# Last V slots of a decoder block taken in another order, with their operands prepared further ahead

## The chip, the cores and the metric

One core of a Trainium2 chip runs the whole program. The metric is the device time of one execution in microseconds (us). PE is TensorE, DVE is VectorE, ACT is ScalarE, SP is the queue that issues the plain DMA transfers; POOL issues the gathers.

## The reference, cut to what matters

The program is a decoder block for 512 tokens and 1024 columns. Its second half is a product-key retrieval over 16384 single-neuron experts, followed by a residual sum and a layer norm:

```python
ub = u[eb]
hb = gelu(einsum('pd,ped->pe', xb, ub))
return einsum('pe,ped->pd', (gb * hb), v[eb])
...
x = layer_norm(ALPHA * x + gate2 * y, ln2_g, ln2_b)
```

Each token uses 128 of the 16384 experts. `gb` is the softmax weight of a chosen expert.

## The kernel before, in words

The 512 tokens are four blocks of 128. Block 0 gathers its rows of `u` and `v` and works through them on DVE, one "unit" (one gathered row per token) at a time, into `y`. Blocks 1 to 3 are computed densely. The experts are cut into 128 **slots** of 128 experts. For slot i, PE first multiplies the U rows by the tokens (`u_mm`), ACT applies gelu into a `stash` tile, and 32 slots later (`LOOK`) PE multiplies the weighted activations by the V rows (`v_mm`), accumulating over all slots in six PSUM banks `yb`: three blocks by two halves of 512 columns. So from slot 96 on only V products are left.

A V slot needs operands that `heads` and `prep` make. Every f32 operand is cut into a high and a low part, so each product is three matmuls (high by high, high by low, low by high). For slot i these are:

- `vraw`: 512 KB of V rows, loaded by SP into one of 3 buffers. A load can start when DVE has read the slot three places earlier.
- `wt`: the dense softmax weights of four slots in one 768 KB load, 2 buffers. Slots 120 to 123 are in chunk 30 and slots 124 to 127 in chunk 31.
- ACT makes the high parts: `vhi` or `uhi` from `vraw` (two buffers each, even slots use v, odd ones u, so slot i needs the matmuls of slot i-4 done), and `ghi` from `gt`. The last four slots, 124 to 127, put their V operands into `h2hi` and `h2lo`, which nothing else uses any more.
- DVE makes `gt` (stash times `wt`), then the low parts: `glo` (2 buffers, so slot i needs slot i-2's matmuls done) and `vlo` or `ulo`. The last `GROUP` = 6 slots put both parts of g into tiles called `glast`, cut from the ring of stash tiles, which need no wait for PE.

`prep(i)` first calls `heads(i)` and `heads(i+1)`; the latter puts the `gt` of slot i+1 into DVE's queue ahead of the `glo` and `vlo` of slot i. Each engine works through its queue in the order in which the program wrote it. How far `prep` runs ahead of `v_mm` in that order is set by `ahead(i)`: two slots, and more for the last three slots before the group.

The last six slots are different: instead of going slot by slot over all banks, PE takes one bank's columns (a **piece**) for all six slots, then the next piece, so that the norm of block 1 can begin while PE is still on blocks 2 and 3. The first piece therefore needs the operands of all six slots. `finish(tb)` is the norm of a block: on DVE for block 0 it is written in five parts (a generator `f0`), one part per slot from slot `LAST` = 115 on. After the last piece, DVE finishes block 3 and SP stores it.

Of the kernel before, what the change touches and what calls it, by code (L numbers as in the profile page):

```python
# [9 lines left out]
F32R = mybir.dt.float32r  # L10
# [10 lines left out]
P = 128  # L21
# [3 lines left out]
TB = 4  # L25
HD = 64
NH = 8
NK = 128
# [7 lines left out]
ND = 384  # L36
TG = 32
NTG = ND // TG
LOOK = 32
WR = 4  # L40
# [4 lines left out]
LEAD = 3  # L45
# [7 lines left out]
BIG = 4  # L53
LAST = 115
GROUP = 6
PRE = 0

CW = 80
# [9 lines left out]
def tile_block(ctx, tc, xr, xT, ccol, wada, bcol, brow, wqk, wv, sinks, gncol, wout,  # L68
# [22 lines left out]
    def split(src, hi, lo, eng=None):  # L91
        A.activation(hi, src, AF.Copy)  # L92
        (eng or V).tensor_tensor(lo, src, hi.bitcast(F32), op=OP.subtract)  # L93

    def load_split(src, shape, tag, pool, eng=None, rawtag=None, rawbufs=None):
        raw = pool.tile(shape, F32, name=f"{tag}raw", tag=rawtag or f"{tag}raw", bufs=rawbufs)
        nc.sync.dma_start(raw, src)
        hi = pool.tile(shape, F32R, name=f"{tag}hi", tag=f"{tag}hi")
        lo = pool.tile(shape, F32R, name=f"{tag}lo", tag=f"{tag}lo")
        split(raw, hi, lo, eng)  # L100
        return hi, lo
# [40 lines left out]
    with ExitStack() as front:  # L142
# [92 lines left out]
        heads = []  # L235
# [283 lines left out]
        for g in range(2):  # L519
            for tb in range(TB):  # L520
                T.matmul(p[:, 4 * g + tb:4 * g + tb + 1], sqa[:, g, tb * P:(tb + 1) * P], ones[:, 0:1], start=True,
                         stop=True, skip_group_check=True)
# [26 lines left out]
        for tb in (1, 2, 3, 0):  # L549
            t = slice(tb * P, (tb + 1) * P)  # L550
            zg = [[ps.tile([P, 512], F32, name="zm", tag="ms"[g]) for _ in range(2)] for g in range(2)]
            for n_c, c in enumerate(ORDER):
                hi, lo = wo[c]
# [51 lines left out]
    mw = mw_cm.__enter__()  # L605

    def bank(tag, nm, shape=(P, 512), bufs=None):
        return ps.tile(list(shape), F32, name=nm, tag=tag, bufs=bufs)
# [33 lines left out]
    for hp in range(NHP):  # L642
        hi, lo = load_split(wq[hp].rearrange("p (c n) -> p c n", c=DC), [P, DC, P], "u", wsp, G)
# [217 lines left out]
    def fetch(n):  # L861
        extra = when[n] > NK - LOOK + 1 and n % 3 == 0
        gat[n] = gather(u_rows, n, extra) if n < P else gather(v_rows, n - P, extra)

    def fetch_to(slot):
        while (n := len(gat)) < 2 * P and when[n] <= slot:
            fetch(n)

    def unit(n):
        t = gat[n]  # L870
        if n < P:
            scr = mw.tile([P, D], F32, name="gscr", bufs=1)
            V.tensor_tensor_reduce(out=scr, in0=t, in1=h2row, scale=1.0, scalar=0.0, op0=OP.mult, op1=OP.add,  # L873
                                   accum_out=hd[:, n:n + 1])
            return
        if n == P:
            A.activation(cf, hd, AF.Gelu_apprx_tanh)
            V.tensor_tensor(cf, cf, g0k, op=OP.mult)
        k = n - P
        if k == 0:  # L880
            V.tensor_scalar(y0, t, cf[:, 0:1], None, op0=OP.mult)
        else:
            V.scalar_tensor_tensor(y0, t, cf[:, k:k + 1], y0, op0=OP.mult, op1=OP.add)  # L883

    mw_cm.__exit__(None, None, None)
    mw = ctx.enter_context(tc.tile_pool(name="mv", bufs=2, reuse_waits="tile"))

    ybank = [[bank(f"y{2 * b + h}", f"yb{b}{h}") for h in range(2)] for b in range(3)]
    uraw, vraw, uop, vop, gop, wts = {}, {}, {}, {}, {}, {}
# [4 lines left out]
            nc.sync.dma_start(uraw[s], uT[s])  # L894

    vseen = set()

    def load_v(i):
        if i < NK and i not in vseen:
            vseen.add(i)  # L900
            vraw[i] = mw.tile([P, D], F32, name="vraw", bufs=3)
            nc.sync.dma_start(vraw[i], v_rows[i * P:(i + 1) * P, :])

    def load_w(c):
        if c < NK // WR:
            w = mw.tile([P, NTG, WR, TG], F32, name="wt")
            nc.sync.dma_start(w.rearrange("p g r t -> p g (r t)"),
                              w_d[:, :, c * WR * TG:(c + 1) * WR * TG].rearrange("g p n -> p g n"))
            wts[c] = w

    def hilo(pool, shape, nm, bufs=2):
        return [pool.tile(shape, F32R, name=f"{nm}{e}", tag=f"{nm}{e}", bufs=bufs) for e in ("hi", "lo")]
# [3 lines left out]
    def weigh(i):  # L916
        if i >= NK or i in gts:
            return
        g = mw.tile([P, NTG, TG], F32, name="gt")
        V.tensor_tensor(g, stash.pop(i).rearrange("p (a t) -> p a t", t=TG), wts[i // WR][:, :, i % WR, :], op=OP.mult)  # L920
        gts[i] = g.rearrange("p a t -> p (a t)")
        gop[i] = [mw.tile([P, ND], F32R, name=f"g{e}", tag=f"g{e}", bufs=k) for e, k in (("hi", 3), ("lo", 2))]             if i < NK - GROUP else [
            ring.tile([P, ND], F32R, name="glast", tag="stash") for _ in range(2)]

    def vtiles(i):
        if i >= NK - 4:
            k = 2 * (i - NK + 4)
            vop[i] = [t[:, k:k + 2].rearrange("p a n -> p (a n)") for t in (h2hi, h2lo)]
        else:
            vop[i] = hilo(wsp, [P, D], "u") if i + LOOK > NK and i % 2 else hilo(mw, [P, D], "v")  # L930

    def heads(i):
        if i < NK and i not in gts:
            vtiles(i)
            A.activation(vop[i][0], vraw[i], AF.Copy)
            weigh(i)
            A.activation(gop[i][0], gts[i], AF.Copy)

    def prep(i, units):
        units = list(units)  # L940
        alone = i + LOOK > NK
        if alone:
            heads(i)
            heads(i + 1)
        elif i < NK:
            weigh(i)
            A.activation(gop[i][0], gts[i], AF.Copy)  # L947
        s = i + LOOK
        if s < NK:
            r = uraw.pop(s).rearrange("p (c n) -> p c n", c=DC)  # L950
            uop[s] = hilo(wsp, [P, DC, P], "u")
            split(r, *uop[s])
        if i < NK:
            if not alone:
                vtiles(i)
            V.tensor_tensor(gop[i][1], gts[i], gop[i][0].bitcast(F32), op=OP.subtract)
            if alone:
                V.tensor_tensor(vop[i][1], vraw.pop(i), vop[i][0].bitcast(F32), op=OP.subtract)
            else:
                split(vraw.pop(i), *vop[i])  # L960
        fetch_to(i + (LEAD if i + LOOK >= NK else 1))
        for n in units:
            unit(n)

# [10 lines left out]
    def v_mm(i, b, cols=((0, 512), (512, 1024))):  # L975
        (hi, lo), (ghi, glo) = vop[i], gop[i]
        t = slice(b * P, (b + 1) * P)
        for n, (x, y) in enumerate(((ghi, hi), (ghi, lo), (glo, hi))):
            for c0, c1 in cols:
                T.matmul(ybank[b][c0 // 512][:, c0 % 512:(c1 - 1) % 512 + 1], x[:, t], y[:, c0:c1],  # L980
                         start=(i == 0 and n == 0),
                         stop=(n == 2 and i == (NK - GROUP - 1 if b == TB - 2 else NK - 1)) or c1 - c0 < 512,
                         skip_group_check=(c1 - c0 < 512))

    plan = [[] for _ in range(NK + 1)]
    todo = list(range(PRE, 2 * P))
    for n, t in enumerate(todo):
# [17 lines left out]
    def pieces(tb):  # L1005
        n = 256 if tb == TB - 1 else 512
        return [(c, c + n) for c in range(0, D, n)]
# [32 lines left out]

    for n in range(min(RING, PRE)):
        fetch(n)
    while len(stash) < LOOK:
        u_slot(len(stash), bank("h", "ph", bufs=2), ring.tile([P, ND], F32, name="stash"), V if len(stash) < LOOK - LG else G)
    for n in range(PRE):
        unit(n)
        if n + RING < PRE:
            fetch(n + RING)
# [13 lines left out]
    def ahead(i):  # L1062
        if i + LOOK < NK:
            return i + 1
        return min(i + 2, NK - GROUP - 1) if i < NK - GROUP - 3 else min(NK, 2 * i - (NK - GROUP) + 8)

    for i in range(NK):
        load_u(i + LOOK + 2)
        load_v(i + 3)
        if i + LOOK >= NK:  # L1070
            load_v(i + 4)
        if i % WR == WR - 1:
            load_w(i // WR + 2)
        p = u_mm(i + LOOK) if i + LOOK < NK else None
        if i < NK - GROUP:
            for b in range(3):
                v_mm(i, b)
        while done <= ahead(i):
            prep(done, plan[done])
            done += 1  # L1080
            if i + LOOK >= NK:
                load_v(done + 1)
                load_v(done + 2)
        if p is not None:
            A.activation(stash[i + LOOK], p[:, :ND], AF.Gelu_apprx_tanh)  # L1085
        if i == NK - LOOK + 1:
            A.preload_act_table_set("natural_log_exp_and_others")

        if i == LAST - 2:
            finish_load(0)  # L1090
        if i == LAST:
            f0 = finish(0)
            finish_ln()
        if i >= LAST:
            next(f0, None)
        if i == NK - GROUP - 1:
            for tb in range(1, TB):
                finish_load(tb)
    for _ in f0:
        pass  # L1100
    for b in range(3):
        for c in pieces(b + 1):
            for i in range(NK - GROUP, NK):
                v_mm(i, b, (c,))
        for _ in finish(b + 1):
            pass
# [70 lines left out]
```

## Time and profile before

| what | us |
|---|---|
| median of 3 runs (1597.34 to 1597.96) | 1597.37 |
| the profiled execution | 1595.99 |
| its span, first to last instruction | 1594.3 |
| PE busy in the span (98%) | 1554.9 |
| DVE busy in the span (77%) | 1220.3 |

The span is what the trace shows; the 1.7 us around it belong to the execution's own time. The profiled execution is 1.4 us under the median of the runs.

### The profile page before, as it was taken

What the parts mean: (1) busy time and instruction counts of PE and PEld (TensorE: products, weight loads), DVE (VectorE), ACT (ScalarE), POOL (GpSimd) and SP (SyncE); (2) the same over time, 40 slices, a digit from 0 to 9 for tenths busy, and PEclk for the clock granted to TensorE, in tenths of its full rate; (3) what the DMA queues carried; (4) which work ended last, traced back from release to release, by engine and by line L of the source; (5) the groups of instructions that cost most, each with busy time, mean ns of one, the idle gap of its engine ahead of it and who ended that gap; (6) DMA issues with size and microseconds to landing.
All of it is one profiled execution on the core that took longest, in us unless ns stands there. A gap on an engine that the chain in (4) does not pass through costs nothing.

```text
span 1594.3 us, 21985 instructions
## 1 busy us (share of the span) xinstructions
PE 1554.9 (98%) x8109; PEld 1346.3 (84%) x8109; DVE 1220.3 (77%) x2351; ACT 647.5 (41%) x935; POOL 455.8 (29%) x410
## 2 busy tenths in 40 slices
PE   8999999999989999999999999999999999999996
PEld 5776767788879999899999999999999999998885
DVE  2568585589999997578777787777877777777878
ACT  2535574333355555333333333333333333333331
POOL 0002133544400000233334333333333444333100
PEclk8999898999999999999999999999999999999999
DMA  9564132222225555999888988999889998989873
GB/s 338 184 258 158 53 112 101 79 92 81 81 80 212 219 210 202 334 327 326 305 311 301 326 301 304 306 309 322 302 303 312 307 321 301 311 282 305 261 231 119
DMA packets 147356, 382.12 MB, mean 240 GB/s; under 512 B 11312, under 2 KB 68656, under 8 KB 143280
## 3 DMA queue, kind: packets, MB, share of 16 engines
q1 hardware_dynamic: 110384, 246.49, 44.6%
q0 software_dynamic: 36864, 134.23, 24.4%
q8 instruction: 63, 1.03, 0.3%
q14 instruction: 45, 0.37, 0.1%
HBM read 351.32 MB, written 29.36 MB: 239 GB/s over the span
## 4 chain that ended last, share of the span: by engine, by line
PE 79%; DVE 12%; DMA 3%; ACT 3%; issue 1%; POOL 1%; SPq 0%; DVEq 0%; ACTq 0%; POOLq 0%
PE yb L980 32%; PE ph L970 25%; PE pw L841 5%; PE ph L806 4%; PE pj L303 3%; PE zm L556 2%; DVE scr L620 1%; PE pj L274 1%; DMA wa<-in_wada_dram 1%; DVE tsi L622 1%; DVE tsi L619 1%; PE pq L647 1%; DVE tsv L621 1%; DVE tsv L618 1%; PE oacc L398 1%
## 5 line engine op out<-in xcount | busy, mean ns | idle before, releaser
L855 POOL DMA_INDIRECT gat<-in_u_rows_dram,idx x128 | 161.6, 1262 | 478.5 <-DVE hd L873 226.5
L93 DVE TENSOR_TENSOR ulo<-uraw,uhi 128x1024 fp32r<-128x1024 f32 x133 | 162.5, 1223 | 164.9 <-ACT uhi L92 160.5
L970 PE MATMUL ph<-h2hi,ulo 128*128 128x384 f32 x768 | 258.6, 337 | 0.6 <-DVE ulo L93 0.6
L970 PE MATMUL ph<-h2hi,uhi 128*128 128x384 f32 x768 | 258.2, 336 | 0.3 <-ACT uhi L92 0.3
L970 PE MATMUL ph<-h2lo,uhi 128*128 128x384 f32 x768 | 258.2, 336 | 0.0
L855 POOL DMA_INDIRECT gat<-in_v_rows_dram,idx x128 | 161.0, 1258 | 264.8 <-DVE y L883 224.1
L980 PE MATMUL yb<-vhi,ghi 128*128 128x512 f32 x654 | 203.0, 391 | 0.0
L980 PE MATMUL yb<-vhi,glo 128*128 128x512 f32 x654 | 202.9, 391 | 0.0
L980 PE MATMUL yb<-vlo,ghi 128*128 128x512 f32 x654 | 202.6, 391 | 0.0
L92 ACT ACTIVATE uhi<-uraw 128x1024 fp32r<-128x1024 f32 x155 | 162.4, 1050 | 74.6 <-PE pq L647 52.9
L883 DVE SCALAR_TENSOR_TENSOR y<-gat,cf,y 128x1024 f32<-128x1024 f32 x127 | 162.7, 1281 | 3.9 <-DMA gat<-in_v_rows_dram,idx 1.6
L873 DVE CUSTOM_DVE_ANT_0 gscr<-gat,h2row 128x1024 f32<-128x1024 f32 x128 | 156.5, 1222 | 10.6 <-DMA gat<-in_u_rows_dram,idx 7.9
L1085 ACT ACTIVATE stash<-ph 128x384 f32<-128x384 f32 x96 | 47.2, 491 | 275.1 <-PE ph L970 275.1
L970 PEld LDWEIGHTS ph<-h2lo,uhi 128*128 128x128 f32 x768 | 144.4, 188 | 4.4
L970 PEld LDWEIGHTS ph<-h2hi,uhi 128*128 128x128 f32 x768 | 144.4, 188 | 4.4 <-ACT uhi L92 0.7
L980 PEld LDWEIGHTS yb<-vlo,ghi 128*128 128x128 f32 x654 | 122.7, 188 | 27.3
L980 PEld LDWEIGHTS yb<-vhi,glo 128*128 128x128 f32 x654 | 122.8, 188 | 26.8
L970 PEld LDWEIGHTS ph<-h2hi,ulo 128*128 128x128 f32 x768 | 144.4, 188 | 1.0 <-DVE ulo L93 1.0
L980 PEld LDWEIGHTS yb<-vhi,ghi 128*128 128x128 f32 x654 | 121.8, 188 | 18.9
L93 DVE TENSOR_TENSOR vlo<-vraw,vhi 128x1024 fp32r<-128x1024 f32 x97 | 118.4, 1220 | 17.5 <-ACT vhi L92 17.4
L92 ACT ACTIVATE vhi<-vraw 128x1024 fp32r<-128x1024 f32 x97 | 102.8, 1060 | 53.6 <-issue 35.8
L947 ACT ACTIVATE ghi<-gt 128x384 fp32r<-128x384 f32 x97 | 51.0, 525 | 177.7 <-DVE gt L920 177.7
(311 smaller groups left out, 2860.1 us busy)
## 6 DMA issues: line engine op xcount, KB each, us to landing
uraw<-in_uT_dram SPq DMA_DIRECT2D x128, 512.0 KB, 5.2
vraw<-in_v_rows_dram SPq DMA_DIRECT2D x128, 512.0 KB, 5.2
w_d<-stage SPq DMA_DIRECT2D x12, 2048.0 KB, 7.3
wt<-w_d SPq DMA_DIRECT2D x32, 768.0 KB, 9.3
wa<-in_wada_dram SPq DMA_DIRECT2D x16, 1024.0 KB, 6.5
wah<-in_wada_dram SPq DMA_DIRECT2D x16, 512.0 KB, 9.4
uraw<-in_wq_dram SPq DMA_DIRECT2D x16, 512.0 KB, 3.3
uraw<-in_wqk_dram SPq DMA_DIRECT2D x11, 512.0 KB, 7.8
```

The lines of the kernel that those rows point to most:

```text
L92: A.activation(hi, src, AF.Copy)
L93: (eng or V).tensor_tensor(lo, src, hi.bitcast(F32), op=OP.subtract)
L303: T.matmul(p, a[:, dc], b[:, dc], start=(dc == 0 and n == 0), stop=(dc == DC - 1 and n == 2))
L806: T.matmul(p[:, :ND], a[:, dc], b[:, dc, P:], start=(dc == 0 and n == 0), stop=(dc == DC - 1 and n == 2))
L841: T.matmul(p[:, k * P:(k + 1) * P], oh4[:, 1, :, k], oh4[:, 2 + j, :, k], start=(j == 0), stop=(j == 1), skip_group_check=True)
L855: G.indirect_dma_start(out=t, out_offset=None, in_=rows, in_offset=bass.IndirectOffsetOnAxis(ap=idx[:, k:k + 1], axis=0))
L873: V.tensor_tensor_reduce(out=scr, in0=t, in1=h2row, scale=1.0, scalar=0.0, op0=OP.mult, op1=OP.add, accum_out=hd[:, n:n + 1])
L883: V.scalar_tensor_tensor(y0, t, cf[:, k:k + 1], y0, op0=OP.mult, op1=OP.add)
L947: A.activation(gop[i][0], gts[i], AF.Copy)
L970: T.matmul(p[:, :ND], a[:, dc], b[:, dc, P:], start=(dc == 0 and n == 0), stop=(dc == DC - 1 and n == 2))
L980: T.matmul(ybank[b][c0 // 512][:, c0 % 512:(c1 - 1) % 512 + 1], x[:, t], y[:, c0:c1], start=(i == 0 and n == 0), stop=(n == 2 and i == (NK ...
L1085: A.activation(stash[i + LOOK], p[:, :ND], AF.Gelu_apprx_tanh)
```

## The change

The last six slots are taken in the order 124, 125, 126, 127, 122, 123 (`seq`), both in `prep` and in the pieces. Slots 114 and later (`OWN` = 14 of them) take both parts of g from the stash ring. `ahead` asks for two slots ahead up to slot 113, for four from slot 114 on, and for all that is left by slot 119. Two parts of the norm of block 0 are written per slot. `prep` also loads the weight chunk of its slots if nobody has yet.

```diff
+OWN = 14
+    seq = list(range(NK - GROUP)) + list(range(NK - 4, NK)) + list(range(NK - GROUP, NK - 4))
...
-    def load_v(i):
-        if i < NK and i not in vseen:
+    def load_v(n):
+        i = seq[min(n, NK - 1)]
+        if n < NK and i not in vseen:
...
-            if i < NK - GROUP else [
+            if i < NK - OWN else [
             ring.tile([P, ND], F32R, name="glast", tag="stash") for _ in range(2)]
...
-    def prep(i, units):
+    def prep(n, units):
         units = list(units)
+        i = seq[n] if n < NK else n
         alone = i + LOOK > NK
         if alone:
-            heads(i)
-            heads(i + 1)
+            for k in (n, n + 1):
+                if k < NK:
+                    load_w(seq[k] // WR)
+                    heads(seq[k])
...
-        return min(i + 2, NK - GROUP - 1) if i < NK - GROUP - 3 else min(NK, 2 * i - (NK - GROUP) + 8)
+        if i < NK - OWN:
+            return i + 2
+        return min(i + 4 + 3 * max(0, i - (NK - GROUP - 5)), NK)
...
         if i >= LAST:
             next(f0, None)
+            next(f0, None)
...
-            for i in range(NK - GROUP, NK):
+            for i in seq[NK - GROUP:]:
                 v_mm(i, b, (c,))
```

First place: SP's queue from the load of block 0's residual (`x1b`) on. Before, with the V loads of slots 116 to 118 in the first row, 119 alone, chunk 30, 120, the two norm vectors `ln`, 121 to 123, chunk 31, and 124 to 127:

```order
L902 DMA vraw<-in_v_rows_dram 128x1024 x3
L998 DMA x1b<-x_d 128x1024
L902 DMA vraw<-in_v_rows_dram 128x1024
L907 DMA wt<-w_d 128x12x128
L902 DMA vraw<-in_v_rows_dram 128x1024
L1003 DMA ln_13768<-in_ln2r_dram 128x1024
L1003 DMA ln_13770<-in_ln2r_dram 128x1024
L902 DMA vraw<-in_v_rows_dram 128x1024 x3
L907 DMA wt<-w_d 128x12x128
L902 DMA vraw<-in_v_rows_dram 128x1024 x4
```

The same place now; the V loads are of slots 116 to 118, then 119 to 121, then 124, 125, 126, and last 127, 122 and 123:

```order
L905 DMA vraw<-in_v_rows_dram 128x1024 x3
L1004 DMA x1b<-x_d 128x1024
L905 DMA vraw<-in_v_rows_dram 128x1024 x3
L910 DMA wt<-w_d 128x12x128
L905 DMA vraw<-in_v_rows_dram 128x1024
L1009 DMA ln_13792<-in_ln2r_dram 128x1024
L1009 DMA ln_13794<-in_ln2r_dram 128x1024
L905 DMA vraw<-in_v_rows_dram 128x1024
L910 DMA wt<-w_d 128x12x128
L905 DMA vraw<-in_v_rows_dram 128x1024
L1045 DMA out_dram<-y_2423 128x512 x2
L905 DMA vraw<-in_v_rows_dram 128x1024 x3
```

Chunk 30 has moved behind the V loads of slots 120 and 121, and chunk 31 stands behind that of slot 125, the second of the last six.

Second place: DVE's queue around the `gt` of slot 120, the first that reads chunk 30, with what each row waits for (DMAHW is a load, PE and Activation an engine). Before, from the first part of block 0's norm on (the `gt` of slots 119 and 120 are the second and the seventh row):

```order
L1019 TENSOR_TENSOR y_2423<-y_2423,gate_76 128x1024
L920 TENSOR_TENSOR gt<-stash,wt 128x384 [waits DVE_49]
L956 TENSOR_TENSOR glo<-gt,ghi 128x384 [waits PE_49,Activation_49]
L958 TENSOR_TENSOR vlo<-vraw,vhi 128x1024 [waits DMAHW1_49]
L1029 SCALAR_TENSOR_TENSOR y_2423<-x1b,y_2423 128x512 [waits DMAHW2_49,DVE_49]
L1030 BN_STATS l2st<-y_2423 128x6 [waits DVE_49]
L920 TENSOR_TENSOR gt<-stash,wt 128x384 [waits DMAHW4_49]
L956 TENSOR_TENSOR glo<-gt,ghi 128x384 [waits PE_49,Activation_49]
L958 TENSOR_TENSOR ulo<-vraw,uhi 128x1024 [waits DMAHW3_49]
```

Now (the `gt` of slots 119 and 120 are the first and the fourth row):

```order
L923 TENSOR_TENSOR gt<-stash,wt 128x384 [waits DVE_49]
L962 TENSOR_TENSOR glast<-gt,glast 128x384 [waits Activation_49]
L964 TENSOR_TENSOR vlo<-vraw,vhi 128x1024 [waits DMAHW1_49,PE_49]
L923 TENSOR_TENSOR gt<-stash,wt 128x384 [waits DMAHW6_49,DVE_49]
L962 TENSOR_TENSOR glast<-gt,glast 128x384 [waits Activation_49]
L964 TENSOR_TENSOR ulo<-vraw,uhi 128x1024 [waits DMAHW3_49,PE_49]
L1025 TENSOR_TENSOR y_2423<-y_2423,gate_76 128x1024
L1035 SCALAR_TENSOR_TENSOR y_2423<-x1b,y_2423 128x512 [waits DMAHW2_49,DVE_49]
L1036 BN_STATS l2st<-y_2423 128x6 [waits DVE_49]
```

The low part of g no longer waits for PE, the low part of V now does, and the first part of the norm of block 0 has moved from behind slot 117 to behind slot 119.

Third place: DVE's queue around the first `gt` that reads chunk 31. Now, from the end of the fourth part of the norm of block 0 on, where the `gt` is that of slot 124, the `glast` and `ulo` are those of slot 121, and the last part of the norm of block 0 follows:

```order
L114 TENSOR_TENSOR l2rs<-l2rs,l2tm 128x1 [waits DVE_49]
L923 TENSOR_TENSOR gt<-stash,wt 128x384 [waits DMAHW3_49]
L962 TENSOR_TENSOR glast<-gt,glast 128x384
L964 TENSOR_TENSOR ulo<-vraw,uhi 128x1024 [waits DMAHW5_49,PE_49]
L1044 SCALAR_TENSOR_TENSOR y_2423<-y_2423,l2rs,ln_13794 128x512 [waits DMAHW1_49,DVE_49]
L1044 SCALAR_TENSOR_TENSOR y_2423<-y_2423,l2rs,ln_13794 128x512
```

Before, the `gt` at that place was that of slot 122, which reads chunk 30:

```order
L113 TENSOR_TENSOR l2rs<-l2rs,l2tm 128x1 [waits DVE_49]
L920 TENSOR_TENSOR gt<-stash,wt 128x384
L956 TENSOR_TENSOR glo<-gt,ghi 128x384 [waits PE_49]
L958 TENSOR_TENSOR ulo<-vraw,uhi 128x1024 [waits DMAHW0_49]
L920 TENSOR_TENSOR gt<-stash,wt 128x384 [waits DVE_49]
```

Chunk 31 is asked for one slot earlier than before: ahead of the low parts of slot 121, where it used to be asked for behind those of slot 122.

## Rows read from the trace of the kernel before

**Rows 1.** Waits from 1400 us on: waiting, awaited, us, times, longest.

```profile
DVE glo L956 <- PE yb L980: 22.8, 24, 2.5
...
PE yb L980 <- DVE h2lo L958: 3.1, 3, 1.2
```

**Rows 2.** PE's timeline, V products: start, us, line, operation, count, idle time before.

```profile
1443.25 0.63 PE L980 MATMUL yb<-vhi,ghi 128*128 128x512 f32 x2
...
1555.33 0.39 PE L980 MATMUL yb<-vhi,glast 128*128 128x512 f32 x1
...
1557.19 0.63 PE L980 MATMUL yb<-h2hi,glast 128*128 128x512 f32 x2
1559.03 0.50 PE L980 MATMUL yb<-h2lo,glast 128*128 128x512 f32 x1 [1.21 <-DVE h2lo L958]
...
1561.10 0.50 PE L980 MATMUL yb<-h2lo,glast 128*128 128x512 f32 x1 [1.10 <-DVE h2lo L958]
...
1562.87 0.49 PE L980 MATMUL yb<-h2lo,glast 128*128 128x512 f32 x1 [0.81 <-DVE h2lo L958]
...
1563.43 0.40 PE L980 MATMUL yb<-vhi,glast 128*128 128x512 f32 x1
...
1567.58 0.39 PE L980 MATMUL yb<-vhi,glast 128*128 128x512 f32 x1
...
1584.32 0.28 PE L980 MATMUL yb<-h2hi,glast 128*128 128x256 f32 x1
```

**Rows 3.** DVE's timeline from the last unit to the first work on PE's result.

```profile
1519.78 1.28 DVE L883 SCALAR_TENSOR_TENSOR y<-gat,cf,y 128x1024 f32<-128x1024 f32 x1
...
1532.29 1.22 DVE L1019 TENSOR_TENSOR y<-y,gate 128x1024 f32<-128x1024 f32 x1
...
1536.39 0.69 DVE L1029 SCALAR_TENSOR_TENSOR y<-x1b,y 128x512 f32<-128x512 f32 x1
...
1537.72 0.54 DVE L920 TENSOR_TENSOR gt<-stash,wt 128x384 f32<-128x384 f32 x1
...
1544.70 0.20 DVE L1033 BATCH_NORM_AGGREGATE l2mv<-l2st 128x2 f32<-128x12 f32 x1
...
1546.85 0.55 DVE L920 TENSOR_TENSOR gt<-stash,wt 128x384 f32<-128x384 f32 x1
...
1548.92 0.55 DVE L920 TENSOR_TENSOR gt<-stash,wt 128x384 f32<-128x384 f32 x1
...
1555.49 1.41 DVE L1038 SCALAR_TENSOR_TENSOR y<-y,l2rs,ln 128x512 f32<-128x512 f32 x2
...
1561.60 1.22 DVE L958 TENSOR_TENSOR h2lo<-vraw,h2hi 128x1024 fp32r<-128x1024 f32 x1
1563.63 0.69 DVE L1027 TENSOR_TENSOR r<-yb,gate 128x512 f32<-128x512 f32 x1 [0.81 <-PE yb L980]
```

**Rows 4.** ACT's timeline: the high part of V of slot 127.

```profile
1559.62 1.06 ACT L935 ACTIVATE h2hi<-vraw 128x1024 fp32r<-128x1024 f32 x1 [1.64 <-DMA vraw<-in_v_rows_dram]
```

**Rows 5.** SP's timeline: the V load of slot 119 and that of chunk 30.

```profile
1528.24 0.33 SPq L902 DMA_DIRECT2D vraw<-in_v_rows_dram  x1
1528.61 0.43 SPq L907 DMA_DIRECT2D wt<-w_d  x1
```

**Rows 6.** DMA landing: `wt` 1520 to 1552, `wt` from 1440, `vraw` from 1490.

```profile
DMA to landing us min/median/max: 5.8/5.8/5.9
...
DMA to landing us min/median/max: 5.8/7.3/9.4
...
DMA to landing us min/median/max: 3.0/3.6/6.8
```

**Rows 7.** Windows: stretch, us, busy PE, PEld, DVE, ACT, POOL, granted clock, DMA share, GB/s.

```profile
23.30:26.30 3.00, 1.10 (x12) 0.97 (x8) 0.94 (x4) 1.28 (x2) 0.00 (x0) 1.00 1.09 354
26.40:33.00 6.60, 5.99 (x14) 4.70 (x15) 3.65 (x4) 2.97 (x5) 0.00 (x0) 0.50 1.09 356
1557.80:1562.90 5.10, 1.98 (x8) 1.00 (x7) 4.93 (x7) 1.65 (x3) 0.00 (x0) 1.00 1.01 370
```

More of the change, by code (lines that the diff above doesn't have):

```diff
@@ L904, in load_w @@
     def load_w(c):
-        if c < NK // WR:
+        if c < NK // WR and c not in wts:
             w = mw.tile([P, NTG, WR, TG], F32, name="wt")
@@ L921, in weigh @@
         gts[i] = g.rearrange("p a t -> p (a t)")
-        gop[i] = [mw.tile([P, ND], F32R, name=f"g{e}", tag=f"g{e}", bufs=k) for e, k in (("hi", 3), ("lo", 2))]             if i < NK - GROUP else [
+        gop[i] = [mw.tile([P, ND], F32R, name=f"g{e}", tag=f"g{e}", bufs=k) for e, k in (("hi", 3), ("lo", 2))]             if i < NK - OWN else [
             ring.tile([P, ND], F32R, name="glast", tag="stash") for _ in range(2)]
@@ L960, in prep @@
                 split(vraw.pop(i), *vop[i])
-        fetch_to(i + (LEAD if i + LOOK >= NK else 1))
+        fetch_to(n + (LEAD if n + LOOK >= NK else 1))
         for n in units:
@@ L981, in v_mm @@
                          start=(i == 0 and n == 0),
-                         stop=(n == 2 and i == (NK - GROUP - 1 if b == TB - 2 else NK - 1)) or c1 - c0 < 512,
+                         stop=(n == 2 and i == (NK - GROUP - 1 if b == TB - 2 else seq[-1])) or c1 - c0 < 512,
                          skip_group_check=(c1 - c0 < 512))
```

## The prediction

> **What bounds the kernel now.** I read the waits of the last 200 us first, then PE's timeline, then that of DVE, ACT and SP at the same place. PE hardly waits for anyone in the last stretch except in three places, 3.1 us in all, each time for DVE's `h2lo` [rows 1]. They lie in the first piece of the last six slots. The slots ahead of it run without a gap: slot 95's V products start at 1443.25 and the group of six at 1555.33, so 27 slots take 4.151 us each [rows 2]. The first piece takes 1563.43 - 1555.33 = 8.10 us, the second, which is the same work, 4.15 [rows 2]. So the stalls and the slow starts behind them cost 3.95 us. This is all that the stretch can give back: 0.25% of the time.
>
> What PE waits for there is the end of DVE's work: the last low part starts at 1561.60, lasts 1.22, and PE uses it at 1562.87 [rows 2, 3]. DVE is late although it has time: from 1400 us on it sat idle 22.8 us in `glo`, which waits for PE to free one of two buffers [rows 1]. After the first piece DVE waits for PE (0.81 us idle at 1563.63, [rows 3]) and everything behind follows PE: the same pieces, the same norms. So the new time is the old one plus the shift of the last low part of V, which is now that of slot 123.
>
> **The change part by part.** The same instructions run; only order, buffers and waits change. `glast` in place of `glo` takes away DVE's wait for PE from slot 114 on. The new wait is for `wt`: I follow it in three steps.
>
> *Step 1, chunk 30.* It now stands in SP's queue behind the V load of slot 121, which needs a buffer that DVE frees with the low part of slot 118. That one needs ACT's high part, whose buffer is free when PE has done slot 114: 1555.33 - 7 x 4.151 = 1526.27, and some 0.2 us for the last matmul (0.40 long, the next starts 0.23 behind it). From the start of a high part to the start of the low part it feeds, the last slot took 1561.60 - 1559.62 = 1.98 us [rows 3, 4]. So the low part of slot 118 runs from about 1528.5 to 1529.7. DVE is free for it by then: even if its last unit starts no sooner than before, at 1519.78, the unit (1.28), four `gt` and three `glo` (0.55 each) and three low parts (1.22) end by 1528.6 with nothing overlapped, and each of these eleven rows starts about 0.08 before the last ends, which brings it to 1527.8 [rows 3]. The V load goes out at 1529.8, chunk 30 another 0.37 later [rows 5], at 1530.15. It lands after 5.8 us [rows 6], at 1535.95. DVE's next row, the `gt` of slot 120, waits for it: DVE idles 6.2 us, more than the three waits it was spared. The low part of slot 119 stands behind it, and PE asks for that only at 1542.9: no stall yet.
>
> *Step 2, chunk 31.* One slot of preparing (`gt`, `glo`, low part) takes 1548.92 - 1546.85 = 2.07 us; the first part of block 0's norm about 1.13 (1.22 less the overlap), the next 1537.72 - 1536.39 = 1.33 [rows 3]. Slot 119, these two, and slot 120 up to the start of its low part (0.94 behind its first row) give 2.07 + 1.13 + 1.33 + 0.94 = 5.47; with 1.22 for the low part, 0.07 for the V load of slot 125 and 0.37 for the weights, chunk 31 goes out 7.1 us after chunk 30 landed, at 1543.05. It lands at 1548.95. DVE has asked since 1546.0: after slot 120 it has only 1.33 and the rest of the norm's middle, 1546.85 - 1544.70 = 2.15 [rows 3].
>
> *Step 3, to the last low part.* From there DVE has slot 121 (2.07), the end of block 0's norm (1.33, [rows 3]), five more slots (10.35), and `glo` of slot 123 (0.47), which starts the last low part 14.22 us later, at 1563.2. But the three V buffers bind a little harder: from the start of one low part to the start of that three places later run 1.22, 0.07, the landing, and 1.98, that is 3.27 plus the landing. The low part of slot 126 starts 8.48 behind chunk 31 (2.07 + 1.33 + 4.14 + 0.94), at 1557.4; with a median landing of 3.6 us [rows 6] that of slot 123 starts at 1564.3. Slot 121's own operands are there at 1551.2, when PE starts it, and its low part is used from the third matmul on: no stall to count.
>
> The sum: 1564.3 - 1561.6 = 2.7 us later. The profiled execution's 1595.99 becomes 1598.7; the median of the runs, 1.38 above it, 1600.1.
>
> *What I do not know.* The landing of `wt`: at least that of the fastest V load, 3.0 us; at most 9.4, seen while gathers were running [rows 6]; I take 5.8, measured twice in just this stretch behind a V load, when no gather ran. The `ln` loads now go out just ahead of chunk 31 and may cost it 0.6. The V landing at the end: 3.0 to 4.0 would move the end from 2.1 to 3.1. The six slots' order, `h2hi` included, costs nothing by itself: those tiles are free. Doubling the parts of the norm per slot adds no work; it is hidden in DVE's waits.
>
> The Trainium skill ("DMA: Bandwidth & Descriptors", section "Anatomy of one DMA") gives a load about 2.0 us fixed plus its bytes at 436 GB/s. For 512 KB that is 3.2, and the trace's 3.0 to 3.6 agrees; for the 768 KB of weights it is 3.8, and the trace has 5.8. By the page's figure the estimate is 1.4 us faster than before, 1596.0; the measurement decides.
>
> **The rivals.**
>
> *B, the weights land as their size says.* Scaled from the fastest V load, 768 KB take 4.5 us. Chunk 30 lands at 1534.65, chunk 31 at 1534.65 + 7.1 + 4.5 = 1546.25, the last low part starts at 1546.25 + 8.48 + 3.27 + 3.6 = 1561.6: no change, 1597.4. For it: chunk 30 meets a queue without the `ln` loads. Against: both rows here. The skill's 3.8 belongs to this case.
>
> *C, faster.* If both chunks landed within 3.0 us, they would be there at 1533.15 and 1543.25, the moment at which DVE asks; the last low part would start at 1558.6, 3.0 us sooner: 1594.4. It decides from landings near 3 us on, and no row has one for `wt`. With no wait at all 3.95 would be had, 1593.4.
>
> *D, the clock falls.* From 1556.7 on PE would do 0.69 us of work for every 2.07 of DVE, over some 8 us. Early in the program PE was busy 1.10 of 3.00 us, and then the granted clock was 0.50 (1.2 in place of 2.4 GHz) for 6.6 us [rows 7]. Against: between 1557.8 and 1562.9 PE was busy 1.98 of 5.10 at clock 1.00 throughout [rows 7]. Half clock over 6.6 us costs 3.3 where PE is busy, less where it waits; I take 2: 1602.1.
>
> **How the numbers follow.** My forecast (A) 68%, B 12%, C 8%, D 12%. The time is that of A, 1600.1; A's own range is 1598.9 to 1601.3 (wt landing from 5.5 to 6.4, V landing 3.0 to 4.0). For 8 in 10 the range must reach B below and most of D above: 1596.6 to 1602.6. About 0.2%, 3.2 us, is what a measurement of this kernel can tell from no change. A lies just inside it: I give 25 of its 68 to slower by more, 43 to the same. D is slower; B is the same; C reaches the bound only where a landing is a little under 3 us or a wait falls away, and counts as faster but for 1. That makes 7% faster, 56% same, 37% slower.
>
> **What would show it.** Right: DVE idle some 6 us in the `gt` of slot 120 and some 3 us in that of slot 124, both put down to `wt`; the waits of `glo` for PE gone behind slot 114; PE with four or five stalls of 1 to 2 us in the first piece, which then takes 10 to 11.5 us; the slots to 121 without a gap. Wrong: a first piece near 4.2 us (then the weights came in time), a gap ahead of 1555 (slot 121 late: chunk 31 landed after 1549.5), or a granted clock of 0.5 in the last 40 us.

## The result, and the profile after

| | before | changed |
|---|---|---|
| median of six runs, us | 1596.59 (1593.75 to 1597.96) | 1604.74 (1603.02 to 1605.43) |
| profiled execution | 1595.99 | 1605.33 |
| its span | 1594.3 | 1603.6 |

The change makes the kernel slower: ratio 1.0051, 95% interval 1.0038 to 1.0063. The forecast was 1600.1 with a range up to 1602.6; the time is 2.1 us outside it.

The code in front of slot 95 is the same in every kernel here, but the time that it took varied from 1433 to 1444 us in the profiled executions. So beside the medians I use the **stretch**: from the first V product of slot 95 to the first product of 256 columns, which stands behind the four pieces of 512 columns. Before it is 1575.83 - 1443.25 = 132.58 us, now 1585.16 - 1442.61 = 142.55, that is +9.97. What follows the stretch lasts 18.4 to 18.5 us in every run.

The waits of the changed kernel from 1400 us on (us in total, times, longest):

```profile
DVE gt L923 <- DMA wt<-w_d: 14.0, 5, 6.5
DVE glo L962 <- PE yb L986: 13.3, 15, 2.5
...
DVE r L1033 <- PE yb L986: 6.0, 4, 4.1
...
PE yb L986 <- DVE ulo L964: 2.7, 2, 1.8
...
PE yb L986 <- DVE h2lo L964: 2.6, 3, 1.1
```

Of the 22.8 us that `glo` waited for PE [rows 1], 13.3 are left, all in front of slot 114. In their place stands a wait for `wt` that the list of before did not show near its top. DVE's timeline says where:

```profile
1535.52 0.56 DVE L923 TENSOR_TENSOR gt<-stash,wt 128x384 f32<-128x384 f32 x1 [6.51 <-DMA wt<-w_d]
...
1550.66 0.56 DVE L923 TENSOR_TENSOR gt<-stash,wt 128x384 f32<-128x384 f32 x1 [4.72 <-DMA wt<-w_d]
...
1551.60 1.22 DVE L964 TENSOR_TENSOR ulo<-vraw,uhi 128x1024 fp32r<-128x1024 f32 x1
...
1559.14 1.22 DVE L964 TENSOR_TENSOR h2lo<-vraw,h2hi 128x1024 fp32r<-128x1024 f32 x1
...
1568.30 1.22 DVE L964 TENSOR_TENSOR ulo<-vraw,uhi 128x1024 fp32r<-128x1024 f32 x1
...
1577.09 0.69 DVE L1033 TENSOR_TENSOR r<-yb,gate 128x512 f32<-128x512 f32 x1 [4.12 <-PE yb L986]
```

The first two rows are the `gt` of slots 120 and 124, the first readers of chunks 30 and 31. The others are the low parts of slots 121, 126 and 123 (the last), and the norm's read of the second piece. Behind slot 95 the last low part starts after 1568.30 - 1442.61 = 125.69 us; before it was 1561.60 - 1443.25 = 118.35 [rows 2, 3]. PE's timeline around it:

```profile
1552.87 0.74 PE L986 MATMUL yb<-ulo,glast 128*128 128x512 f32 x2 [1.76 <-DVE ulo L964]
...
1556.71 0.39 PE L986 MATMUL yb<-h2hi,glast 128*128 128x512 f32 x1
...
1560.42 0.50 PE L986 MATMUL yb<-h2lo,glast 128*128 128x512 f32 x1 [1.11 <-DVE h2lo L964]
...
1562.00 0.79 PE L986 MATMUL yb<-h2hi,glast 128*128 128x512 f32 x1 [0.85 <-ACT glast L940]
1563.73 0.79 PE L986 MATMUL yb<-h2lo,glast 128*128 128x512 f32 x1 [0.94 <-DVE h2lo L964]
...
1566.37 0.80 PE L986 MATMUL yb<-vlo,glast 128*128 128x512 f32 x1 [0.93 <-DVE vlo L964]
...
1569.58 0.79 PE L986 MATMUL yb<-ulo,glast 128*128 128x512 f32 x1 [0.93 <-DVE ulo L964]
...
1570.59 0.63 PE L986 MATMUL yb<-h2hi,glast 128*128 128x512 f32 x1
...
1576.89 0.40 PE L986 MATMUL yb<-h2hi,glast 128*128 128x512 f32 x1
```

Slot 121 stalls, and the first piece lasts 1570.59 - 1556.71 = 13.88 us in place of 8.10, with stalls for slots 125, 126, 127, 122 and 123. The second piece waits for nothing and still takes 6.30 us, before 4.15: the same matmuls show 0.63 and 0.79 us where they showed 0.39 and 0.50 [rows 2]. The windows give the clock (stretch, us, PE's busy time, granted clock, DMA share, GB/s):

```profile
1555.00:1560.00 5.00, 3.77 (x16) 1.00 0.77 259
1560.00:1565.00 5.00, 2.80 (x6) 0.66 0.81 256
1565.00:1570.00 5.00, 2.88 (x5) 0.50 0.70 252
1570.00:1575.00 5.00, 5.00 (x13) 0.50 0.01 3
1575.00:1580.00 5.00, 5.00 (x23) 0.98 0.02 3
```

The granted clock fell to 0.50 (1.2 GHz) among the stalls and came back at about 1575, within the second piece, which has no gap. Last, SP's timeline of the loads, and how long the loads took to land: both chunks, then the last four V loads (issued from 1552.9 to 1560.4), which by themselves took 3.8, 4.2, 4.7 and 5.8.

```profile
1529.45 0.43 SPq L910 DMA_DIRECT2D wt<-w_d  x1
1537.77 0.33 SPq L905 DMA_DIRECT2D vraw<-in_v_rows_dram  x1
1538.21 1.10 SPq L1009 DMA_DIRECT2D ln<-in_ln2r_dram  x2
1542.41 0.33 SPq L905 DMA_DIRECT2D vraw<-in_v_rows_dram  x1
1542.79 0.42 SPq L910 DMA_DIRECT2D wt<-w_d  x1
1552.89 0.33 SPq L905 DMA_DIRECT2D vraw<-in_v_rows_dram  x1
1553.51 1.01 SPq L1045 DMA_DIRECT2D out_dram<-y  x2
1556.28 4.48 SPq L905 DMA_DIRECT2D vraw<-in_v_rows_dram  x3
1560.87 1.31 SPq L1004 DMA_DIRECT2D x1b<-x_d  x3
```

```profile
DMA to landing us min/median/max: 6.0/6.9/7.8
...
DMA to landing us min/median/max: 3.8/4.4/5.8
```

### The profile page after: what moved, and what is told of

Same layout as the page of the kernel before. It is cut to its first block, busy times and chain, and to the rows that moved or that the text cites. A ratio compares the mean times of both kernels' runs of the same rounds, so it can differ in the third digit from the quotient of the medians.

```text
span 1603.6 us, 21978 instructions
## 1 busy us (share of the span) xinstructions
PE 1558.3 (97%) x8109; PEld 1347.1 (84%) x8109; DVE 1220.0 (76%) x2351; ACT 647.8 (40%) x935; POOL 452.2 (28%) x410
## 4 chain that ended last, share of the span: by engine, by line
PE 79%; DVE 12%; DMA 4%; ACT 3%; issue 1%; POOL 1%; SPq 0%; DVEq 0%; ACTq 0%; POOLq 0%
PE yb L986 31%; PE ph L976 25%; PE pw L842 6%; PE ph L807 5%; PE pj L304 3%; PE zm L557 2%; DVE scr L621 1%; DMA wa<-in_wada_dram 1%; PE pj L275 1%; DVE tsi L623 1%; DVE tsi L620 1%; DMA wt<-w_d 1%; PE pq L648 1%; DVE tsv L622 1%; DVE tsv L619 1%
## 5 line engine op out<-in xcount | busy, mean ns | idle before, releaser
L856 POOL DMA_INDIRECT gat<-in_u_rows_dram,idx x128 | 158.2, 1236 | 481.7 <-DVE hd L874 237.6
L986 PE MATMUL yb<-vhi,ghi 128*128 128x512 f32 x630 | 195.6, 391 | 0.0
L986 PE MATMUL yb<-vhi,glo 128*128 128x512 f32 x630 | 195.5, 391 | 0.0
L986 PE MATMUL yb<-vlo,ghi 128*128 128x512 f32 x630 | 195.2, 391 | 0.0
L986 PEld LDWEIGHTS yb<-vlo,ghi 128*128 128x128 f32 x630 | 118.2, 188 | 26.4
L986 PEld LDWEIGHTS yb<-vhi,glo 128*128 128x128 f32 x630 | 118.3, 188 | 25.8
L986 PEld LDWEIGHTS yb<-vhi,ghi 128*128 128x128 f32 x630 | 117.3, 188 | 17.9
```

The source lines that it names most:

```text
L856: G.indirect_dma_start(out=t, out_offset=None, in_=rows, in_offset=bass.IndirectOffsetOnAxis(ap=idx[:, k:k + 1], axis=0))
```

## The experiments

The theories, by the letters that the expectations use. **W**: the loss is DVE's wait for the two chunks, and behind it the gain is there. **V**: the last V loads and their three buffers bind anyway. **S**: the order of the six slots costs. **L**: the `ln` loads just ahead of chunk 31 delay it. **K**: PE's stalls let the clock fall, which costs some 2 us by itself. **G**: what stalled the kernel before was `glo`'s wait for PE. **Q** and **K2** come last.

**e1, both chunks loaded early; e2 and e3, one of them.** In the loop over the slots, behind `prep(done)`:

```diff
+            if done == 114:
+                load_w(30)
+            if done == 118:
+                load_w(31)
```

> The changed kernel with the loads of chunks 30 and 31 written as soon as their buffers are free (behind the preparing of slots 114 and 118), and nothing else. Theory W (the loss comes from DVE waiting for these two loads, 6.5 and 4.7 us after the change): both waits gone, the first piece of the last six slots takes about 4.2 us, the clock stays at 1.00, and the whole is 3.9 us faster than the kernel before, near 1592.7. Rival V (the last V loads, which took 4.2 to 5.8 us after the change, and their three buffers bind by themselves): DVE's waits move to the V loads, the first piece still takes 8 us or more, 1597 or later. Rival S (taking slots 124 to 127 first costs by itself): same as V in time, with PE waiting for slots 122 and 123.

> The changed kernel with only chunk 30 loaded early; chunk 31 stays behind the V load of slot 125. Theory W: DVE's 6.5 us wait in the gt of slot 120 is gone, but the low part of slot 120 is then bound by PE (slot 116 done), so chunk 31 goes out about 5 us sooner than after the change and the wait in the gt of slot 124 remains, 4 to 8 us long. Last low part about 5 us sooner, and with the clock kept 2 us more: 1597 to 1599.5. Rival V: the time stays within 2 us of the changed kernel (1602.7 or more).

> The changed kernel with only chunk 31 loaded early; chunk 30 stays behind the V load of slot 121. Theory W: the 6.5 us wait in the gt of slot 120 remains, the 4.7 us wait in that of slot 124 is gone, the last low part comes 4 to 5 us sooner, 1598 to 1600.5, less if the clock still falls. If the two waits simply add up, this and the kernel with only chunk 30 early together save as much as both early do; if one hides behind the other, less. Rival V: within 2 us of the changed kernel.

| | ratio to before (95%) | stretch, us | waits for `wt` at slots 120, 124 |
|---|---|---|---|
| changed | 1.0051 (1.0038 to 1.0063) | 142.55 | 6.51, 4.72 |
| e1, both early | 0.9962 (0.9947 to 0.9977) | 128.80 | none, none |
| e2, chunk 30 early | 0.9997 (0.9984 to 1.0011) | 133.81 | none, 3.21 |
| e3, chunk 31 early | 1.0011 (0.9996 to 1.0026) | 138.35 | 8.93, none |

In e1 the changed kernel becomes faster than the kernel before: median 1591.91 against 1596.52. PE's timeline has no stall in the pieces, and the clock stays (windows of e1):

```profile
1550.00:1555.00 5.00, 5.00 (x23) 1.00 0.89 282
1555.00:1560.00 5.00, 5.00 (x22) 1.00 0.56 213
1560.00:1565.00 5.00, 5.00 (x23) 1.00 0.02 5
```

W holds. V and S fall as causes that act by themselves; what the last V loads add once chunk 31 is late is e9's question. In the stretch e2 saves 8.74 us, e3 4.20 and e1 13.75, so the two waits nearly add up. Chunk 30 is the larger half, since all that DVE does for the slots behind stands behind its wait, chunk 31's load too: with chunk 30 in time, chunk 31 goes out 4.5 us sooner. In e3 chunk 31 stands ahead of chunk 30 in the queue, and slot 120 waits 8.93 in place of 6.51: a chunk moved ahead delays the other.

**e4, nothing but the stash tiles for g.** The kernel before, in `weigh`:

```diff
-            if i < NK - GROUP else [
+            if i < NK - 14 else [
```

> The kernel before with one part of the change alone: slots 114 and later take both parts of g from the stash ring; order of slots, preparing ahead and the norm of block 0 as before. Theory W: DVE no longer waits for PE in glo, SP's queue still has chunk 30 behind the V load of slot 119 and chunk 31 behind that of slot 123, DVE is ahead of both; the stalls of the first piece go, about 3.9 us faster than before, 1592.7. If instead DVE's lead is eaten by waits for V loads or weights, between 1593 and 1597.

Ratio 0.9945 (0.9924 to 0.9966), median 1590.93; stretch 130.57; the clock stays at 1.00. Two stalls are left where none was expected, 0.17 and the one of this row (PE's timeline of e4):

```profile
1560.59 0.50 PE L980 MATMUL yb<-h2lo,glast 128*128 128x512 f32 x1 [1.23 <-DVE h2lo L958]
```

G holds in the main: by the medians this one line alone is as fast as e1, without the order, the preparing further ahead and the doubled norm. It takes away ACT's wait for PE in `ghi` together with DVE's in `glo`; the two were not tried apart. In the stretch it gives 2.0 of the 3.8 us that e1 gives. DVE waits 1.14 us for chunk 30 here and not at all for chunk 31, so these tiles alone make neither load late enough to matter; the rest of the change does.

**e7, e1 with the slots in their natural order**, `seq = list(range(NK))`.

> Both chunks early, as in the kernel without stalls, but the last six slots in their old order 122 to 127. Theory W: the order is worth nothing once the weights are there, stretch 128.5 to 129.5, same as with both chunks early. Rival S: the V operands of slots 126 and 127 come too late in the old order, one or two stalls, 130 to 132.

Ratio 0.9982 (0.9969 to 0.9995), stretch 129.48, one stall of 0.55 us. The order is worth 0.7 us of the stretch in this pair of executions: S has the wrong sign, and the size is within what one execution can differ by. The intervals of the two ratios, this one's and e1's, just overlap.

**e8, the kernel before with both chunks early**, with the lines of e1.

> The kernel before with both chunks loaded early and nothing else: glo still has two buffers and waits for PE. Theory G (the stalls of the kernel before come from DVE's wait for PE in glo): nothing changes, stretch 132 to 133. Rival: weights were late there too, stretch below 131.5.

Ratio 1.0004 (0.9991 to 1.0016). The waits of `glo` (2.04, 0.81, 0.72, 0.62) and PE's stalls (1.21, 1.10, 0.83, 0.93) are still those of the kernel before, so early weights alone bring nothing. But the stretch is 136.27, with the granted clock at 0.72 and 0.60 behind the stalls, which the profiled execution of before did not show. e10 and e11 follow this up.

**e5, the `ln` loads two slots earlier**: `finish_ln()` moved to the slot in which block 0's residual is loaded, so that they stand ahead of chunk 30.

> The changed kernel with the two norm vectors ln loaded two slots sooner, so that they no longer stand just ahead of chunk 31 in SP's queue. I measure the stretch from the first V product behind the last U product to the first matmul of 256 columns: 132.6 us before, 142.6 after the change, 128.8 with both chunks early. Theory L (chunk 31 took 7.8 in place of 5.9 us because it shared the DMA engines with ln): it lands 5.8 to 6.2 us after its issue, the last low part comes 1.5 to 2.5 us sooner, the stretch is 140 to 141. Rival: chunk 31 is slow for another reason, 7.5 us or more again, stretch as after the change.

Chunk 31 lands in 5.7 us in place of 7.8 (the landing of `wt` in e5 from 1535 to 1545 us): L holds.

```profile
DMA to landing us min/median/max: 5.7/5.7/5.7
```

But chunk 30 now takes 8.7 in place of 6.0, slot 120 waits 9.28, and the stretch is 142.79: nothing is won. The `ln` loads delay chunk 30 now, through the three V loads between them: these took 8.6, 7.8 and 6.0 us, in the changed kernel 3.7, 4.0 and 3.9, and chunk 30 went out as long behind slot 95 as there. The ratio is 1.0047 (1.0030 to 1.0063). The Trainium skill ("DMA: Bandwidth & Descriptors", section "Queues, rings and completion order") says that the transfers of one queue are taken in order of its ring on each DMA engine; this pair of landings agrees. The order does not settle a landing by itself, though. In the trace of before, three V loads stood 3.8 us behind a load of weights, those of slots 120, 116 and 124; the first went out 0.49 us ahead of the `ln` loads, the others had none near (landings in us, last number):

```profile
vraw<-in_v_rows_dram SPq DMA_DIRECT2D x1, 512.0 KB, 5.5
...
vraw<-in_v_rows_dram SPq DMA_DIRECT2D x1, 512.0 KB, 3.5
...
vraw<-in_v_rows_dram SPq DMA_DIRECT2D x1, 512.0 KB, 3.3
```

So the `ln` loads, which spread one row over 128 partitions, also slow a load that is issued just ahead of them.

**e6, the changed kernel with 12 dead matmuls**: three each ahead of the second product of slots 126, 127, 122 and 123 in the first piece. They write a bank that nobody reads any more and are no part of the reference's work.

```diff
+    junk = bank("h", "ph", bufs=2)
...
+            for _ in range(fill if n == 1 else 0):
+                T.matmul(junk[:, :512], gop[seq[-6]][0][:, :P], vop[seq[-6]][0][:, :512], start=True, stop=True)
...
-                v_mm(i, b, (c,))
+                v_mm(i, b, (c,), 3 if b == 0 and c[0] == 0 and i not in (124, 125) else 0)
```

> The changed kernel with three more matmuls (128 by 128 by 512, into a bank that nothing reads; they are not part of the reference's work) put in front of the second matmul of slots 126, 127, 122 and 123 in the first piece, that is into PE's waits. Theory K (the waits of PE make the clock fall, which costs what the second piece takes above 4.15 us, 2.1 us): the granted clock stays 1.00, the second piece takes 4.15 us, the stretch is 140 to 141, and the whole about 2 us faster than the changed kernel. If the clock falls all the same, the stretch is as after the change or up to 3 us longer.

With more work the kernel is faster than the changed one: ratio to before 1.0016 (1.0003 to 1.0029), stretch 140.27. The waits for `wt` (6.43, 5.04) and slot 121's stall (2.00) are about as they were. The clock isn't (windows of e6, the columns as above):

```profile
1560.00:1565.00 5.00, 3.22 (x12) 1.00 0.87 290
1565.00:1570.00 5.00, 2.98 (x11) 1.00 0.49 192
1570.00:1575.00 5.00, 5.00 (x23) 1.00 0.02 5
```

K holds: the fall of the clock costs 2.3 us by itself, 142.55 - 140.27. The last low part came no sooner than in the changed kernel (DVE's timeline of e6; its slot 95 begins at 1441.68):

```profile
1567.74 1.22 DVE L964 TENSOR_TENSOR ulo<-vraw,uhi 128x1024 fp32r<-128x1024 f32 x1
```

From this row to the end of the stretch it is 14.21 us, in the kernel before 132.58 - 118.35 = 14.23, in the changed one 142.55 - 125.69 = 16.86: behind the last low part the clock is the whole difference.

**e9, a quiet queue behind chunk 31.** Theory Q: the last V loads landed late because of the transfers around them. The `x1b` loads of blocks 1 to 3 now take `vraw` buffers, so that they go out behind the last V loads, and block 0's result is stored behind them.

```diff
-        fin[tb] = mw.tile([P, D], F32, name="x1b", tag="gat", bufs=RING)
+        fin[tb] = mw.tile([P, D], F32, name="x1b", tag="vraw", bufs=3) if tb else mw.tile([P, D], F32, name="x1b", tag="gat", bufs=RING)
...
-        for d in (slice(0, 512), slice(512, 1024)):
+        halves = (slice(0, 512), slice(512, 1024))
+        for d in halves:
...
-            nc.sync.dma_start(out[t, d], r[:, d])
+            if tb:
+                nc.sync.dma_start(out[t, d], r[:, d])
+        if tb == 0:
+            while "go" not in fin:
+                yield
+            for d in halves:
+                nc.sync.dma_start(out[t, d], r[:, d])
...
+    fin["go"] = True
```

> The changed kernel with nothing but V loads in SP's queue behind chunk 31: the x1b loads of blocks 1 to 3 go out behind the low parts of the last slots, and the stores of block 0's result behind the last V load. Theory Q (the four last V loads landed after 3.8, 4.2, 4.7 and 5.8 us because other transfers stood around them): they land in 3.0 to 3.7, the last low part starts some 2 us sooner, and the stretch from slot 95's V product to the first matmul of 256 columns is 139.5 to 141 us against 142.6; the median about 1602.5. Rival: the landings are set by something else, stay at 3.8 to 5.8, and the stretch is 142 to 143.

Ratio 1.0034 (1.0021 to 1.0047), median 1602.14, stretch 139.04. In its trace SP issues the four V loads from 1552.44 to 1559.98; the first and the last end ACT's waits here (ACT's timeline of e9):

```profile
1555.82 1.07 ACT L938 ACTIVATE h2hi<-vraw 128x1024 fp32r<-128x1024 f32 x1 [1.09 <-DMA vraw<-in_v_rows_dram]
...
1563.33 1.06 ACT L938 ACTIVATE uhi<-vraw 128x1024 fp32r<-128x1024 f32 x1 [0.83 <-DMA vraw<-in_v_rows_dram]
```

So both landed within 3.4 us, where the changed kernel has 3.8 and 5.8. From the `gt` of slot 124 (1550.21) to the last low part (1565.31) it is 15.10 us; in the changed kernel 1568.30 - 1550.66 = 17.64. Q holds, with 2.5 us, and the stretch is below the 139.5 us expected. The `x1b` loads and the stores were moved together, so which of them counts is not shown. The rest of the gain in the stretch is mostly chunk 31, which slot 124 waited for 4.04 us here.

**e10 and e11, the kernel before twice more; e12, the changed one once more.** Theory K2: the kernel before loses to the clock too, in some of its executions.

> The kernel before, one more execution. Theory K2 (its own stalls in the first piece sometimes let the clock fall, as in e8): the stretch is 132.6 us where the clock stays at 1.00 and 135 to 137 where it falls to 0.50. Rival (the fall in e8 came from its early weights): the stretch is 132 to 133 in each execution and the clock stays.

> As e10_before_again, a further execution: by theory K2 the stretch is either 132.6 or 135 to 137 us, by the rival 132 to 133.

> The changed kernel, one more execution. Theory: the stalls of its last stretch are set by the order of its loads, so DVE waits again 6 to 7 us for chunk 30 and 4 to 5 us for chunk 31, slot 121 stalls by 1 to 2.4 us, the clock falls behind 1560, and the stretch is 142 to 143 us. Rival: these waits vary from one execution to the next by more than 1 us, or the clock stays and the stretch is near 140.3.

K2 holds. The stretches of before are 135.87 and 136.14, with stalls of 1.77, 1.09, 0.85 and 1.26, 1.10, 0.81, 0.93. The windows of e10:

```profile
1555.00:1560.00 5.00, 3.23 (x15) 1.00 0.88 276
1560.00:1565.00 5.00, 3.06 (x9) 0.72 0.88 343
1565.00:1570.00 5.00, 5.00 (x15) 0.60 0.02 5
1570.00:1575.00 5.00, 5.00 (x24) 1.00 0.00 0
```

e12 repeats the changed kernel: waits of 6.41 and 4.44 for the chunks, 1.38 us of stall at slot 121, the clock at 0.50, and a stretch of 141.86, just under what was expected.

## Why the prediction had the path right and three terms wrong

In the profiled executions, counted from slot 95's first V product:

| step | predicted, us | measured, us |
|---|---|---|
| `gt` of slot 120 starts | 92.70 | 92.91 |
| from there to the `gt` of slot 124 | 13.00 | 15.14 |
| from there to the last low part | 15.35 | 17.64 |
| last low part, against 118.35 before | +2.7 | +7.34 |
| behind it, against before | 0 | +2.63 |

The misses are 0.21, 2.14, 2.29 and 2.63 us, together the 7.27 from +2.7 to +9.97: the landing of chunk 31, the landing of the last V load, and the clock.

**Step 1 was right.** Chunk 30 went out at 1529.45, DVE waited 6.51 us (forecast 6.2), and PE asked for nothing late there.

**Step 2 failed in one term: the landing of chunk 31.** It was taken as 5.9 us from two loads behind a single V load, with 0.6 more named as possible because of the `ln` loads. DVE's work from chunk 30 to the issue was 7.27 us against 7.1. The landing was 7.8, and e5 shows that the `ln` loads make the difference. The order of the queue had shown them there; they were given 0.6 us, where 7.8 against the 5.7 of e5 is 2.1, and left out of the sum, though each of the two is as large as a V load, and though V loads beside them had taken 5.5 and 5.2 us in the trace of before. By the Trainium skill's figure ("DMA: Bandwidth & Descriptors", section "Anatomy of one DMA") the load would take 3.8 as an estimate; the page gives that figure for transfers that GpSimd issues, these are SP's, and the two measured landings, 6.0 and 7.8, don't agree with it. Rival B, which had 4.5 from the fastest V load, had no ground here either.

With that, slot 121 was not in time: the step said there was no stall to count, and PE waited 1.76 us. By itself this costs nothing, as PE waits for the last low part further on; whether it helped the clock to fall, no run shows.

**Step 3 was right in its rule and failed in the V landing.** From the `gt` of slot 124 to the low part of slot 126 the forecast was 8.48, and the trace has 1559.14 - 1550.66 = 8.48. Then the chain through the buffers bound, as the step said, but the last load landed in 5.8 us and not in the median 3.6. The forecast allowed 3.0 to 4.0 here, while the row it took them from goes up to 6.8 [rows 6]. e9 shows why: with `x1b` loads and stores out of the way both ends of that chain land within 3.4, and the 15.35 become 15.10. The step didn't ask what else its queue would carry just then: the stores of block 0 among the four V loads, the `x1b` loads 0.43 us behind the last.

**Rival D was treated as another case, but it came with A.** It was given 12% and 2 us on top. The size was about right (2.63 in the profile, 2.28 by e6's stretch), the chance was not. Its counter-evidence was one stretch of the profiled execution of before, PE busy 1.98 of 5.10 us at clock 1.00 [rows 7]. e10 and e11 have almost the same stalls and the clock fell. One execution showed that the clock can stay there, not that it does. Among the profiled executions the clock stayed in e1 (no stall), e7 (one), e4 (two) and e6 (dead matmuls in the waits); it fell in e2, e3, e5, e9 and both of the changed kernel (three to eight stalls); with the three or four stalls of the kernel before it fell in three of four, e8 counted. By these counts the four or five stalls that A forecast made D the likelier case.

**The reading of the kernel before was right.** PE's stalls there come for the larger part from DVE's idle time in `glo` (e4 takes it away, with ACT's wait in `ghi`, and nothing else; of 3.12 us of stalls 1.40 are left), and 3.95 us is what the profiled stretch could give back: e1 gives 132.58 - 128.80 = 3.78. Of the signs named in advance, DVE's 6 us at slot 120 and the vanished waits of `glo` came; stalls in the first piece came too, seven of 0.26 to 1.11 us in place of four or five of 1 to 2; some 3 us at slot 124 (4.72), a first piece of 10 to 11.5 us (13.88) and slots to 121 without a gap did not. Of those for a wrong forecast two came: a gap ahead of 1555, and the clock at 0.5.

The medians differ by 8.15 us, the profiled stretches by 9.97. The execution of before from which the forecast was made is one whose clock stayed, and the other two of the three profiled executions took 3.3 and 3.6 us more. That fits, and also why e4's median gains more than the 2.0 us of its stretch against 132.58. How often it falls in runs without a profile was not measured, and the time in front of slot 95 varies by more than this difference.

The best version measured in the stretch is e1; by median and ratio e1 and e4 can't be told apart.

## What to carry to other kernels

When an operation is put further ahead, list what else sits in the same queue in front of its load and just behind it, and price the landing by that; a landing measured behind one load doesn't hold behind three. Removing a wait pays only if no new one takes its place: here the buffers alone gained (e4), and the preparing further ahead in a new order, which put the loads of weights behind more V loads, lost more than that until these loads were moved too (e1). Where PE is left half idle in short gaps, ask for the clock in several executions, and count its loss as part of the stall, not as another case.

## What the runs showed of the hardware that was not expected

- The same 768 KB load landed in 5.7 to 6.0 us behind one 512 KB load in the kernel before, the changed one and e5, in 7.8 behind one and two `ln` loads just ahead of it, and in 8.7 as chunk 30 in e5, three V loads behind the `ln` loads. In e4, with a V load and the `ln` loads issued within 2.7 us behind it, DVE waited for it until 7.3 us after its issue.
- In the kernel before and in the changed one the granted clock fell to 0.50 among stalls of at most 1.8 us each, and not in every execution: in the kernel before it stayed at 1.00 with stalls of 1.21, 1.10 and 0.81 and fell with 1.26, 1.10, 0.81 and 0.93 (e11). In the changed kernel, after it had fallen, work that takes 4.15 us at the higher level took 6.3 without a gap.
- Twelve matmuls of no use, put into the stalls, made the kernel 2.3 us faster in the stretch.
